# Attention scores over 128 rows, block adds tied together, and low parts of weight tiles on GpSimd

## The chip, the cores and the metric

The kernel runs on one core of one Trainium2 chip. The metric is the device time of one launch in microseconds (us). A core has TensorE (matrix products; PE in the profile, and PEld for its weight loads), VectorE (DVE), ScalarE (ACT), GpSimd (POOL) and SyncE (SP, which starts most transfers). Each runs its own list of instructions in order and waits for the others by semaphores.

## The reference

Two transformer blocks on 256 tokens of width 1024. The first adds three branches: a gated recurrence (lru), a sparse attention (nsa) and a gated linear attention (gla), then merges them and ends with an FFN. The second has two layers with a context of 256 more tokens; the even one has a windowed attention, the odd one a neighbourhood attention. All heads have 64 features.

```python
def nsa_mixer(q, kv, gate, rel_table, cmp_pos, cmp_w1, cmp_w2):
    ...
    blocks = jnp.concatenate([ch[:, :, j:j + n_cmp] for j in range(r)], axis=3) + pos_emb   # compress_blocks
    ...
    logit = jnp.einsum("bgrqd,bgqnld->bgrqnl", qb, ks).astype(f32) + bias
    ...
    logit_w = jnp.einsum("bgrnqd,bgnkd->bgrnqk", qw, kw).astype(f32) + bias_w
def rglru_mixer(...):
    u = jnp.sqrt(-jnp.expm1(2.0 * log_a)) * (i * xc.astype(f32))
    ...
    return h.astype(xa.dtype) * jax.nn.gelu(ga)
def window_gqa(q, k, v, k_ctx, v_ctx, sink):
    ...
    s_ctx = jnp.einsum('bnqkgd,bckd->bnkgqc', qb, k_ctx).astype(jnp.float32) * scale
def neighbourhood_attn(q, k, v, k_ctx, v_ctx, rpb):
    ...
    s_ctx = jnp.einsum('bmqhd,bchd->bhmqc', qr, k_ctx).astype(jnp.float32) * scale
```

## The kernel before

**Weights.** Every large product is done in three parts to keep float32 accuracy. `Core.wload` (L63) brings a weight tile of 128x1024 by a transfer on SP into `wraw`, ScalarE rounds it to `wh` (L74), and VectorE makes the low part `wl = wraw - wh` (L75). Each of the three has a ring of three buffers. `mm3` (L109) then issues `wh` x high, `wl` x high (L114, L115) and `wh` x low (L118) on TensorE. `wload` has an argument `low` for the engine of the subtraction; with none it is VectorE, and the subtraction is entered in `self.lows`, behind which the small adaLN products (L1131) are queued.

**Sparse attention.** `Block1.run` (L1006) weaves it with the recurrent branch: `K.weave(seq, nsa, NS)` runs a list of 44 projection units (each loads one weight tile: four of a gla output, sixteen of the two lru halves, sixteen merges, eight of a branch), and 0.83 steps of the attention after each. The attention has 32 items (8 chunks of heads x 2 query tiles x 2 heads). An item's step issues the score of item i (L645), the transposes of item i-2 (L667) and the values of item i-3 (L686). A score takes 64 of the 128 rows, since a chunk holds two heads:

```python
hs = slice(s * 64, s * 64 + 64)
nc.tensor.matmul(sps, self.qT[hs, ci, t * P:t * P + P], self.kT[hs, a, :, 0:nk], start=True, stop=True)
```

The keys `kT` are copied by ScalarE in `k_unit` (L489), long before. In an lru half GpSimd does the inner part of a gelu (L147 to L149) and a square (L783) per unit, and VectorE a convolution (L757, L760) and the products L784 and L786.

**Blocks.** `blocks` (L515) adds a position table to the tokens of the sparse attention's compressed keys in 8 VectorE additions of 128x8x15 for each of two calls (L526), rounds the result on ScalarE and takes the rest on VectorE. `K.fill(1)` in `run` issues one piece of the adaLN work ahead.

**Even and odd attention.** The even layer's scores (L1556) are 32 items, 16 with 512 keys and 16 with 256; the keys are turned on TensorE and copied by ScalarE (`turned_k`, L1517). The odd layer's (L1788) are 16 items with 512 keys; its queries are turned and copied (L1767). Both are woven with projection units; in the odd layer with 4 tiles of 1024 columns and 8 of 512.

**Order.** The instructions are issued in the order of the program, and a scheduler of the tile framework then orders each engine's list by dependencies, priorities and the rings' free buffers. The ring `a4` of `Block1` has 8 buffers, and holds among others the keys, the values, the block sums and the recurrence's arrays.

Of the kernel before, what the change touches and what calls it, by code (L numbers as in the profile page):

```python
# [14 lines left out]
P = 128  # L15
# [9 lines left out]
class Core:  # L25
    def __init__(self, tc, ctx, D):
        self.tc, self.nc, self.D = tc, tc.nc, D
        self.cp = ctx.enter_context(tc.tile_pool(name="const", bufs=1))
        self.yp = ctx.enter_context(tc.tile_pool(name="big", bufs=2))
        self.wp = ctx.enter_context(tc.tile_pool(name="wstream", bufs=3))  # L30
        self.sp = ctx.enter_context(tc.tile_pool(name="small", bufs=2))
        self.pp = ctx.enter_context(tc.tile_pool(name="psum", bufs=4, space=PSUM))
        self.n = 0
        self.ready, self.lows = {}, []

        self.filler, self.rate, self.credit = [], 0.0, 0.0
        nc = self.nc
        self.ident = self.cp.tile([P, P], F32, name="ident")
        nc.scalar.dma_start(self.ident, D["ident"])
        self.ones = self.cp.tile([P, P], F32, name="ones")  # L40
        nc.vector.memset(self.ones, 1.0)

        ps = self.psum("at")
        for _ in range(WARM):
            nc.tensor.matmul(ps[:, :P], self.ones, self.ones, start=True, stop=True)
        self.power = self.cp.tile([P, 8], F32, name="power")
        nc.gpsimd.memset(self.power, -0.5)
        self.ng = self.cp.tile([P, 32], F32, name="ng")
        nc.scalar.dma_start(self.ng, D["ng"])
# [11 lines left out]
                self.ready[key] = self.wload(src, src.shape[-1], False, low, parts)  # L61

    def wload(self, src, cols, take=True, low=None, parts=1):  # L63
        nc = self.nc
        key = src.tensor.name, src.offset
        if take and key in self.ready:
            return self.ready.pop(key)
        raw = self.wp.tile([P, 1024], F32, tag="wraw", name=self.nm("wraw"))
        h = self.wp.tile([P, 1024], F32R, tag="wh", name=self.nm("wh"))
        l = self.wp.tile([P, 1024], F32R, tag="wl", name=self.nm("wl"))  # L70
        for i in range(parts):
            c = slice(i * cols // parts, (i + 1) * cols // parts)
            nc.sync.dma_start(raw[:, c], src[:, c])
            nc.scalar.copy(h[:, c], raw[:, c])  # L74
            i = (low or nc.vector).tensor_tensor(out=l[:, c], in0=raw[:, c], in1=h.bitcast(F32)[:, c],  # L75
                                                 op=ALU.subtract)
        if low is None:
            self.lows = (self.lows + [i.ins.name])[-LOOSE:]
        self.credit += self.rate
        while self.credit >= 1.0:  # L80
            self.credit -= 1.0
            self.fill(1)
        return h, l
# [247 lines left out]
class Block1:  # L331
# [156 lines left out]

    def k_unit(self, br, a):  # L489
        if br == a == 0:  # L490
            self.kT = self.a4("kT", shape=(P, 2, 2, 256))
        self.nc.scalar.copy(self.kT[:, a, br, :], self.proj_t(12 + 2 * br + a))

    def v_units(self):
        self.vN = self.a4("vN", shape=(P, 2, 512))
# [19 lines left out]
    def blocks(self, kv):  # L515

        nc = self.nc
        x2r = self.x2[kv].rearrange("p g (c s) -> p s g c", s=16)
        flat = self.a4("blk", shape=(P, 1024))
        bh = self.a8("blkh", F32R, (P, 1024))  # L520
        bl = self.a8("blkl", F32R, (P, 1024))
        nc.gpsimd.memset(flat[:, 960:], 0.0)
        blk = flat[:, :960].rearrange("p (i g c) -> p i g c", i=16, g=4)
        for ih in range(2):
            for g in range(4):
                nc.vector.tensor_tensor(  # L526
                    out=blk[:, 8 * ih:8 * ih + 8, g, :], in0=x2r[:, 0::2, g, ih:ih + 15],
                    in1=self.cpos[:, kv, 8 * ih:8 * ih + 8][:, :, None].to_broadcast([P, 8, 15]), op=ALU.add)
        nc.scalar.copy(bh, flat)
        nc.vector.tensor_tensor(out=bl, in0=flat, in1=bh.bitcast(F32), op=ALU.subtract)  # L530
        self.blk.append((bh, bl))

# [71 lines left out]
    def nsa_steps(self):  # L604
# [35 lines left out]
        def scores(ci, t, s):  # L640
            a, r = divmod(ci, 4)
            g, nk = 2 * a + s, (t + 1) * P
            sps = K.psum("mm")[:, :2 * nk].rearrange("p (b n) -> p b n", b=2)
            hs = slice(s * 64, s * 64 + 64)
            nc.tensor.matmul(sps, self.qT[hs, ci, t * P:t * P + P], self.kT[hs, a, :, 0:nk], start=True, stop=True)  # L645
            pr = self.s1("t2", (P, 512)).rearrange("p (b n) -> p b n", b=2)[:, :, :nk]
            nc.vector.tensor_tensor(out=pr, in0=sps, in1=Bs[ci][:, s:s + 1, 256 - nk:].to_broadcast([P, 2, nk]),
                                    op=ALU.add)
            mx = self.s1("mx", (P, 2))
            nc.vector.tensor_reduce(out=mx, in_=pr, axis=AX.X, op=ALU.max)  # L650
            nc.vector.tensor_scalar(out=mx, in0=mx, scalar1=-1.0, scalar2=None, op0=ALU.mult)
            sm = self.s1("sm", (P, 2))
            for b in range(2):
                nc.scalar.activation(pr[:, b, :], pr[:, b, :], AF.Exp, bias=mx[:, b:b + 1], accum_out=sm[:, b:b + 1])
            nc.vector.reciprocal(sm, sm)
            nc.vector.tensor_tensor(out=sm, in0=sm, in1=gv[:, t, 1:3, g, r], op=ALU.mult)
            for b in range(2):
                nc.vector.tensor_scalar(out=pr[:, b, :], in0=pr[:, b, :], scalar1=sm[:, b:b + 1], scalar2=None,
                                        op0=ALU.mult)
            prs[ci, t, s] = pr  # L660
# [345 lines left out]
    def run(self):  # L1006
# [9 lines left out]
        k = [(lambda br=br, a=a: self.k_unit(br, a)) for br in range(2) for a in range(2)]  # L1016
        self.gates_turned()
        self.nsa_rows()
        K.fill(1)
        for f in q[2:5]:  # L1020
            f()
        self.blocks(0)
        for f in q[5:]:
            f()
        self.blocks(1)
        decay = self.gla_decay()

        def mixed(a, b):
# [50 lines left out]
        K.rate = 0.0  # L1079
        seq = b2[4:] + l0 + [then(l1[0], *a0)] + l1[1:] + [then(mg[0][0], *a1)] + mg[0][1:6]  # L1080
        seq += [then(mg[0][6], ysplit), mg[0][7]] + b0 + mg[1]
        K.weave(seq, nsa, NS)
        for _ in nsa:
            pass
        K.rate = RATE_GLA
# [141 lines left out]
class Block2:  # L1227
# [224 lines left out]
    def even(self, l, z, norm, ahead):  # L1452
# [50 lines left out]
        for f in self.proj_units(z, W[0:4], 512, X, to(q), z.steps(1)):  # L1503
            f()
        qT = K.big("qT", shape=(P, 4, 512))
        kT = self.t("kT", (P, 512))

        def turned_q(ts):
            for c in range(0, 4, 2):
# [7 lines left out]
        def turned_k(ts):  # L1517
            ps = K.psum("at")
            for n, t in enumerate(ts):
                nc.tensor.transpose(ps[:, n * P:n * P + P], k[:, t, :], K.ident)  # L1520
            nc.scalar.activation(kT[:, ts[0] * P:ts[-1] * P + P], ps[:, :len(ts) * P], AF.Copy,
                                 scale=1.0 if ts == X else gc[:, 1:2])

        def heads():
            yield from self.head_norm(q, X, 8)
# [25 lines left out]
        def score(item, pr):  # L1551
            t, keys, h = item
            c, s = divmod(h, 2)
            hs = slice(s * 64, s * 64 + 64)
            ps = K.psum("mm")[:, :len(keys) * P]
            nc.tensor.matmul(ps, qT[hs, c, t * P:(t + 1) * P], kT[hs, keys[0] * P:keys[-1] * P + P], start=True,  # L1556
                             stop=True)
            parts = [(ps[:, :256], mask[:, t, :]), (ps[:, 256:], None)] if t < 2 else [(ps, None)]
            return self.softmax(parts, (sink[:, h:h + 1], nsink[:, h:h + 1]), pr)
# [177 lines left out]
    def odd(self, l, z, norm, ahead):  # L1737
# [25 lines left out]
        K.weave(vu, heads(), 1)  # L1763
        kT = K.big("qT", shape=(P, 4, 512))
        self.to_T(k, 4, 4, lambda c, ps: nc.scalar.activation(kT[:, c, :], ps, AF.Copy, scale=gc[:, 1:2]))
        qT = self.t("e4", (P, 4, 256))
        self.to_T(q, 2, 4, lambda c, ps: nc.scalar.activation(qT[:, c, :], ps, AF.Copy, scale=gc[:, 0:1]))  # L1767
        y = (self.t("hh", (P, 8, 256), F32R), self.t("hl", (P, 8, 256), F32R))

        items = [(t, (0, 1, 2, 3), h) for t in range(2) for h in range(8)]  # L1770
# [8 lines left out]
        def score(item, pr):  # L1779
            t, keys, h = item  # L1780
            c, s = divmod(h, 2)
            hs = slice(s * 64, s * 64 + 64)
            if (t, c) not in Bs:
                bias(t, c)
            if s == 0 and t * 4 + c < 7:
                bias(*divmod(t * 4 + c + 1, 4))
            ps = K.psum("mm")
            nc.tensor.matmul(ps, qT[hs, c, t * P:(t + 1) * P], kT[hs, c, :], start=True, stop=True)  # L1788
            return self.softmax([(ps[:, :256], Bs[t, c][:, s, :]), (ps[:, 256:], None)], None, pr)
        prb = self.t("n8", (P, 4, 512), bufs=2)  # L1790
        ptb = self.t("wsT", (P, 2, 512))
# [3 lines left out]
        def pooled(g):  # L1795
# [13 lines left out]
            self.split_evac(y, g, 0, 256, t)  # L1809
            yield  # L1810
        pools = (None for g in range(4) for _ in pooled(g))
        K.weave(self.proj_units(z, W[12:16], 512, X, to(xp)), att, OD)
        K.weave([lambda: next(pools, None)] * 8 + self.out_units(l, K.D["od_o"], y, 256, range(4)), att, OD2)
        for _ in att:
            pass
        return self.out_proj(l, K.D["od_o"], y, 256, norm, ahead, range(4, 8))
# [312 lines left out]
```

## Time and profile before

| what | us |
|---|---|
| median of 3 runs (lowest to highest) | 2393.02 (2391.76 to 2394.91) |
| the profiled execution | 2392.35 |
| its span | 2390.6 |
| busy: TensorE | 2354.4 (98%) |
| busy: VectorE | 1710.8 (72%) |
| busy: ScalarE | 1051.4 (44%) |
| busy: GpSimd | 175.4 (7%) |

The span runs from the first instruction to the last, in one profiled execution; the execution's own time has 1.75 us more around it. The busy shares are averages over stages with different limits, so a stage is read from its own window. Matmuls overlap at their ends, so the distance between two starts tells what one takes, rather than its own duration. PEclk is the granted clock of TensorE, 1.00 for 2.4 GHz and 0.50 for 1.2 GHz.

### The profile page before, as it was taken

To read this page: it belongs to the slowest core of one execution; us is meant where nothing else is said; L and a number is where in the kernel's file an instruction comes from. 1 tells how busy PE (TensorE), PEld (TensorE's weight loads), DVE (VectorE), ACT (ScalarE), POOL (GpSimd) and SP (SyncE) were. 2 spreads that over 40 slices of the span, in tenths; PEclk is the share of its full clock that TensorE was granted. 3 is DMA by queue.
4 is the path that set the end of the run, shared out by engine and by line. 5 is a ranking of instruction groups with operands and counts; after the bars stand their busy time and mean duration, and the time that the engine had idled before them with its cause. 6 is when DMAs were issued, how large, how long until landed. Compare 5 with 4: busy or idle time off the path is not lost.

```text
span 2390.6 us, 38670 instructions
## 1 busy us (share of the span) xinstructions
PE 2354.4 (98%) x14647; PEld 2065.6 (86%) x14647; DVE 1710.8 (72%) x3621; ACT 1051.4 (44%) x1839; POOL 175.4 (7%) x203
## 2 busy tenths in 40 slices
PE   8999999999999999999999999999999999999999
PEld 8888988999999988888778888888988888878999
DVE  7976898789899964458767765656865643846666
ACT  5532576465445422236755322223522223656443
POOL 1000120010000000003321000000100000100000
PEclk9999999999999999999999999999999999999999
DMA  7773533567886755545214644544653532534554
GB/s 241 244 238 113 161 110 117 152 221 239 268 267 215 258 178 162 168 132 162 94 58 136 208 154 129 162 140 137 208 165 126 155 111 90 182 119 132 185 180 157
DMA packets 158310, 398.91 MB, mean 167 GB/s; under 512 B 27131, under 2 KB 41371, under 8 KB 158123
## 3 DMA queue, kind: packets, MB, share of 16 engines
q1 hardware_dynamic: 157835, 396.35, 52.8%
q8 instruction: 115, 1.88, 0.3%
q14 instruction: 72, 0.59, 0.1%
q10 hardware_dynamic: 288, 0.08, 0.0%
HBM read 389.56 MB, written 5.77 MB: 165 GB/s over the span
## 4 chain that ended last, share of the span: by engine, by line
PE 82%; DVE 8%; DMA 4%; ACT 2%; issue 2%; POOL 1%; SPq 0%; ACTq 0%; DVEq 0%; POOLq 0%
PE ps_mm L114 23%; PE ps_mm L118 22%; PE ps_mm L115 22%; DVE wl L75 3%; PE ps_mm L1315 2%; PE ps_mm L1316 2%; PE ps_mm L1317 2%; DMA wraw<-in_up 2%; DVE junk L1131 1%; PE ps_at L1422 1%; ACT wh L74 1%; PE ps_mm L645 1%; PE ps_mm L1556 1%; DMA wraw<-in_w_in_t 1%; PE ps_at L1411 1%
## 5 line engine op out<-in xcount | busy, mean ns | idle before, releaser
L74 ACT CAST wh<-wraw 128x1024 fp32r<-128x1024 f32 (+2 forms) x605 | 605.4, 1001 | 735.8 <-PE ps_mm L118 369.9
L75 DVE TENSOR_TENSOR wl<-wraw,wh 128x1024 fp32r<-128x1024 f32 (+2 forms) x605 | 707.5, 1170 | 264.3 <-ACT wh L74 248.6
L114 PE MATMUL ps_mm<-zh,wh 128*128 128x256 f32 (+2 forms) x2512 | 751.3, 324 | 7.2 <-ACT wh L74 5.9
L115 PE MATMUL ps_mm<-zh,wl 128*128 128x256 f32 (+2 forms) x2512 | 746.8, 322 | 6.5 <-DVE wl L75 6.4
L114 PEld LDWEIGHTS ps_mm<-zh,wh 128*128 128x128 f32 x2512 | 477.8, 190 | 62.4 <-issue 12.7
L115 PEld LDWEIGHTS ps_mm<-zh,wl 128*128 128x128 f32 x2512 | 478.3, 190 | 49.9 <-DVE wl L75 9.2
L118 PE MATMUL ps_mm<-zl,wh 128*128 128x256 f32 (+2 forms) x2512 | 448.0, 321 | 0.0
L118 PEld LDWEIGHTS ps_mm<-zl,wh 128*128 128x128 f32 x2512 | 373.7, 190 | 38.5 <-issue 0.3
L1131 DVE SCALAR_TENSOR_TENSOR junk<-araw,cs 128x512 f32<-128x512 f32 x576 | 391.4, 691 | 10.8 <-DMA araw<-in_ada_w 3.8
L114 PE MATMUL ps_mm<-hh,wh 128*128 128x256 f32 (+1 forms) x1021 | 313.0, 329 | 1.9 <-ACT wh L74 0.9
L115 PE MATMUL ps_mm<-hh,wl 128*128 128x256 f32 (+1 forms) x1021 | 311.3, 327 | 1.0 <-DVE wl L75 1.0
L114 PEld LDWEIGHTS ps_mm<-hh,wh 128*128 128x128 f32 x1021 | 192.8, 189 | 23.1 <-ACT hh L300 1.6
L115 PEld LDWEIGHTS ps_mm<-hh,wl 128*128 128x128 f32 x1021 | 193.0, 189 | 20.3 <-DVE wl L75 1.6
L118 PE MATMUL ps_mm<-hl,wh 128*128 128x256 f32 (+1 forms) x1021 | 194.1, 328 | 0.2 <-DVE hl L301 0.2
L118 PEld LDWEIGHTS ps_mm<-hl,wh 128*128 128x128 f32 x1021 | 156.6, 189 | 18.9 <-DVE hl L301 0.4
L298 ACT ACTIVATE silu<-ps_mm 128x512 f32<-128x512 f32 (+1 forms) x102 | 50.2, 493 | 261.1 <-PE ps_mm L118 242.7
L1261 DVE SCALAR_TENSOR_TENSOR X<-ps_mm,adac,X 128x256 f32<-128x256 f32 x128 | 61.9, 483 | 133.9 <-PE ps_mm L118 132.8
L299 DVE TENSOR_TENSOR silu<-silu,ps_mm 128x512 f32<-128x512 f32 (+1 forms) x102 | 56.6, 555 | 105.8 <-PE ps_mm L118 105.8
L126 POOL TENSOR_TENSOR rs_v<-rs_v,power 128x2 f32<-128x2 f32 (+1 forms) x17 | 24.1, 1418 | 1291.4 <-ACT wh L74 713.5
L1315 PE MATMUL ps_mm<-wh,zh 128*128 128x512 f32 (+1 forms) x224 | 87.3, 390 | 0.0
L1316 PE MATMUL ps_mm<-wh,zl 128*128 128x512 f32 (+1 forms) x224 | 86.0, 384 | 0.0
L1317 PE MATMUL ps_mm<-wl,zh 128*128 128x512 f32 (+1 forms) x224 | 85.6, 382 | 0.0
(399 smaller groups left out, 2661.2 us busy)
## 6 DMA issues: line engine op xcount, KB each, us to landing
wraw<-in_up SPq DMA_DIRECT2D x204, 512.0 KB, 3.7
araw<-in_ada_w SPq DMA_DIRECT2D x288, 256.0 KB, 3.4
wraw<-in_w_in_t SPq DMA_DIRECT2D x70, 512.0 KB, 3.6
wraw<-in_dn SPq DMA_DIRECT2D x79, 448.0 KB, 3.3
wraw<-in_f_up SPq DMA_DIRECT2D x44, 512.0 KB, 4.4
wraw<-in_dn SPq DMA_DIRECT2D x40, 512.0 KB, 3.6
wraw<-in_ev_in SPq DMA_DIRECT2D x26, 512.0 KB, 3.5
wraw<-in_w_br SPq DMA_DIRECT2D x24, 512.0 KB, 3.8
```

Source lines behind the costliest of these rows:

```text
L74: nc.scalar.copy(h[:, c], raw[:, c])
L75: i = (low or nc.vector).tensor_tensor(out=l[:, c], in0=raw[:, c], in1=h.bitcast(F32)[:, c], op=ALU.subtract)
L114: nc.tensor.matmul(out, wh, ah, start=start and k == 0, stop=False)
L115: nc.tensor.matmul(out, wl, ah, start=False, stop=False)
L118: nc.tensor.matmul(out, wh, al, start=False, stop=stop and k == n - 1)
L298: nc.scalar.activation(g, p0, AF.Silu)
L299: nc.vector.tensor_tensor(out=g, in0=g, in1=ps, op=ALU.mult)
L1131: K.behind(nc.vector.scalar_tensor_tensor(out=junk, in0=raw, scalar=1.0, in1=self.cs[:, s, h * 512:(h + 1) * 512], op0=ALU.mult, op1=ALU.mult,
L1261: self.nc.vector.scalar_tensor_tensor(out=X[:, m, :], in0=ps, scalar=self.ada.c[l][:, j, m, s:s + 1], in1=X[:, m, :], op0=ALU.mult, op1=AL ...
L1315: nc.tensor.matmul(ps[i], z.zh[:, k, tk], wh[:, w], start=k == 0, stop=False)
L1316: nc.tensor.matmul(ps[i], z.zl[:, k, tk], wh[:, w], start=False, stop=False)
L1317: nc.tensor.matmul(ps[i], z.zh[:, k, tk], wl[:, w], start=False, stop=k == 7)
```

## The change

Three edits. First, each score is a product over all 128 rows. One of the two operands exists twice, once for each head of the chunk, with zeros in the other head's 64 rows, so that the sum over 128 rows is the same. GpSimd writes the zeros. In the odd layer the queries are doubled, elsewhere the keys. Second, the 8 block additions of a call become 2 of 128x480, the rounding that follows is kept in its place in the program, and `K.fill(1)` comes after the blocks. Third, `Core.low` names the engine of the low parts: GpSimd while the sparse attention and the two weaves of the odd layer are issued, 44 and 12 tiles. Line numbers of the changed kernel are some 2 to 25 higher.

```diff
@@ wload
-        nc = self.nc
+        nc, low = self.nc, low or self.low
@@ k_unit
-            self.kT = self.a4("kT", shape=(P, 2, 2, 256))
-        self.nc.scalar.copy(self.kT[:, a, br, :], self.proj_t(12 + 2 * br + a))
+            self.kT = [self.a4("kT", shape=(P, 2, 2, 256)) for s in range(2)]
+            for s in range(2):
+                self.nc.gpsimd.memset(self.kT[s][(1 - s) * 64:(1 - s) * 64 + 64], 0.0)
+        ps = self.proj_t(12 + 2 * br + a)
+        for s in range(2):
+            hs = slice(s * 64, s * 64 + 64)
+            self.nc.scalar.copy(self.kT[s][hs, a, br, :], ps[hs])
@@ blocks
-            for g in range(4):
-                nc.vector.tensor_tensor(
-                    out=blk[:, 8 * ih:8 * ih + 8, g, :], in0=x2r[:, 0::2, g, ih:ih + 15],
-                    in1=self.cpos[:, kv, 8 * ih:8 * ih + 8][:, :, None].to_broadcast([P, 8, 15]), op=ALU.add)
-        nc.scalar.copy(bh, flat)
+            nc.vector.tensor_tensor(
+                out=blk[:, 8 * ih:8 * ih + 8], in0=x2r[:, 0::2, :, ih:ih + 15],
+                in1=self.cpos[:, kv, 8 * ih:8 * ih + 8][:, :, None, None].to_broadcast([P, 8, 4, 15]), op=ALU.add)
+
+        self.K.tc.keep_in_program_order(nc.scalar.copy(bh, flat))
@@ nsa_steps, scores
-            hs = slice(s * 64, s * 64 + 64)
-            nc.tensor.matmul(sps, self.qT[hs, ci, t * P:t * P + P], self.kT[hs, a, :, 0:nk], start=True, stop=True)
+            nc.tensor.matmul(sps, self.qT[:, ci, t * P:t * P + P], self.kT[s][:, a, :, 0:nk], start=True, stop=True)
@@ Block1.run
-        K.fill(1)
...
         self.blocks(1)
+        K.fill(1)
...
+        K.low = K.nc.gpsimd
         K.weave(seq, nsa, NS)
+        K.low = None
@@ even attention
-        kT = self.t("kT", (P, 512))
+        kT = [self.t("kT", (P, 512)), k.rearrange("p t n -> p (t n)")]
...
-            nc.scalar.activation(kT[:, ts[0] * P:ts[-1] * P + P], ps[:, :len(ts) * P], AF.Copy,
-                                 scale=1.0 if ts == X else gc[:, 1:2])
+            cols = slice(ts[0] * P, ts[-1] * P + P)
+            for s in range(2):
+                hs, other = slice(s * 64, s * 64 + 64), slice((1 - s) * 64, (1 - s) * 64 + 64)
+                nc.gpsimd.memset(kT[s][other, cols], 0.0)
+                nc.scalar.activation(kT[s][hs, cols], ps[hs, :len(ts) * P], AF.Copy,
+                                     scale=1.0 if ts == X else gc[hs, 1:2])
...
-            nc.tensor.matmul(ps, qT[hs, c, t * P:(t + 1) * P], kT[hs, keys[0] * P:keys[-1] * P + P], start=True,
+            nc.tensor.matmul(ps, qT[:, c, t * P:(t + 1) * P], kT[s][:, keys[0] * P:keys[-1] * P + P], start=True,
@@ odd attention
-        qT = self.t("e4", (P, 4, 256))
-        self.to_T(q, 2, 4, lambda c, ps: nc.scalar.activation(qT[:, c, :], ps, AF.Copy, scale=gc[:, 0:1]))
+        e4, ge = self.t("e4", (P, 4, 256)), [self.t("gelu", (P, 512), bufs=2) for _ in range(2)]
+        qT = [[e4[:, c, :] for c in range(4)], [ge[c // 2][:, c % 2 * 256:c % 2 * 256 + 256] for c in range(4)]]
+        nc.gpsimd.memset(e4[64:128], 0.0)
+        for g in ge:
+            nc.gpsimd.memset(g[0:64], 0.0)
+        def turned_q(c, ps):
+            for s in range(2):
+                hs = slice(s * 64, s * 64 + 64)
+                nc.scalar.activation(qT[s][c][hs], ps[hs], AF.Copy, scale=gc[hs, 0:1])
+        self.to_T(q, 2, 4, turned_q)
...
-            nc.tensor.matmul(ps, qT[hs, c, t * P:(t + 1) * P], kT[hs, c, :], start=True, stop=True)
+            nc.tensor.matmul(ps, qT[s][c][:, t * P:(t + 1) * P], kT[:, c, :], start=True, stop=True)
...
+        K.low = nc.gpsimd
         K.weave(self.proj_units(z, W[12:16], 512, X, to(xp)), att, OD)
         K.weave([lambda: next(pools, None)] * 8 + self.out_units(l, K.D["od_o"], y, 256, range(4)), att, OD2)
+        K.low = None
```

How the engines' lists change is shown at two places. The first is GpSimd's list in the first lru half, one unit; `t` is the unit's gelu, `lv` the square of the recurrence's factor, `lc` a buffer of the compressed scores. Before:

```order
L147 TENSOR_TENSOR t_606_3233<-t_601_3200 128x256
L754 MEMSET t_614_3266 128x4
L148 TENSOR_SCALAR t_606_3233<-t_606_3233 128x256
L149 TENSOR_TENSOR t_606_3233<-t_606_3233,t_601_3200 128x256
L621 MEMSET lc_3853 128x2x8
```

With the change, the same unit (L149 to L151 are now the gelu, L789 the square):

```order
L789 TENSOR_TENSOR lv_2983<-la_2984 128x256
L628 MEMSET lc_3848 128x2x8
L149 TENSOR_TENSOR t_607_3228<-t_602_3195 128x256
L760 MEMSET t_615_3261 128x4
L150 TENSOR_SCALAR t_607_3228<-t_607_3228 128x256
L151 TENSOR_TENSOR t_607_3228<-t_607_3228,t_602_3195 128x256
L77 TENSOR_TENSOR wl_3409<-wraw_3407,wh_3408 128x1024
L77 TENSOR_TENSOR wl_3513<-wraw_3511,wh_3512 128x1024
```

Two low parts, of tiles that TensorE uses two tiles later, stand behind each gelu, and the next unit's work behind them. The transfers into `wraw`, queued on SP, wait for GpSimd's readers of the buffer instead of VectorE's.

The second is VectorE's list in the second lru half; `lu` is the recurrence's input, `sm` and `t` with 128x256 x2 belong to a softmax, `convw` to the convolution. Before, the product L786 of a unit stands in the midst of it:

```order
L757 TENSOR_SCALAR t_709_3749<-t_704_3715,convw,lruv 128x256
L75 TENSOR_TENSOR wl_3886<-wraw_3884,wh_3885 128x1024
L655 RECIPROCAL sm_3708<-sm_3708 128x2
L760 SCALAR_TENSOR_TENSOR t_709_3749<-t_704_3715,convw,t_709_3749 128x256
L656 TENSOR_TENSOR sm_3708<-sm_3708,nsagate 128x2
L786 SCALAR_TENSOR_TENSOR lu_3556<-t_711_3757,t_680_3594 128x256
L658 TENSOR_SCALAR t_701_3703<-t_701_3703,sm_3708 128x256 x2
```

With the change the same products (now L792) of all four units stand together, after the last gelu of the half (L154):

```order
L154 SCALAR_TENSOR_TENSOR lg_3552<-t_781_4108,t_776_4075 128x256
L656 TENSOR_REDUCE mx_4127<-t_786_4125 128x2
L657 TENSOR_SCALAR mx_4127<-mx_4127 128x2
L661 RECIPROCAL sm_4130<-sm_4130 128x2
L662 TENSOR_TENSOR sm_4130<-sm_4130,nsagate 128x2
L664 TENSOR_SCALAR t_786_4125<-t_786_4125,sm_4130 128x256 x2
L792 SCALAR_TENSOR_TENSOR lu_3551<-t_712_3752,t_681_3589 128x256
L792 SCALAR_TENSOR_TENSOR lu_3551<-t_746_3919,t_710_3744 128x256
L792 SCALAR_TENSOR_TENSOR lu_3551<-t_767_4035,t_744_3911 128x256
L681 COPY pct_4197<-ps_at_4195 128x128
L792 SCALAR_TENSOR_TENSOR lu_3551<-t_795_4173,t_765_4027 128x256
```

The `wl` rows are gone from VectorE's list, and the four `lu` products moved behind the half's last gelu: the second `kT` holds a buffer of the ring `a4` that `lu` took before, so `lu` waits for another to come free. What the products read (`t`, buffers of the ring that the softmax uses too) is held until then.

## Rows read from the trace of the kernel before

**Rows 1.** Page, busy time of the engines, share of the span, instructions.

```profile
PE 2354.4 (98%) x14647; PEld 2065.6 (86%) x14647; DVE 1710.8 (72%) x3621; ACT 1051.4 (44%) x1839; POOL 175.4 (7%) x203
```

**Rows 2.** Windows: us; busy PE, PEld, DVE, ACT, POOL (instructions); PEclk, DMA, GB/s.

```profile
275.00:360.00 85.00, 83.16 (x592) 72.70 (x592) 79.38 (x214) 61.04 (x155) 26.18 (x42) 1.00 0.39 118
360.00:447.00 87.00, 86.67 (x642) 76.55 (x642) 70.96 (x200) 50.93 (x129) 7.21 (x10) 1.00 0.37 114
1130.00:1240.00 110.00, 107.72 (x544) 77.84 (x543) 73.16 (x236) 76.14 (x201) 37.52 (x34) 0.98 0.24 77
2115.00:2168.00 53.00, 53.00 (x282) 37.23 (x281) 24.38 (x95) 31.18 (x77) 0.00 (x0) 1.00 0.23 68
```

**Rows 3.** Timeline of PE: start, us, line, operation, out<-in, rows*columns, columns, number.

```profile
284.00 0.39 PE L683 MATMUL ps_at<-pct,vc 128*128 128x128 f32 x2
284.22 1.06 PE L686 MATMUL ps_at<-t,vN 128*128 128x128 f32 x8
285.21 0.70 PE L645 MATMUL ps_mm<-kT,qT 64*128 64x256 f32 x2
285.83 0.38 PE L114 MATMUL ps_mm<-zh,wh 128*128 128x256 f32 x1
```

**Rows 4.** Timeline of PE, 128 rows and 256 columns (lru gates).

```profile
333.97 1.02 PE L775 MATMUL ps_at<-t,lruw 128*128 128x256 f32 x4
334.83 0.38 PE L667 MATMUL ps_at<-ident,t 128*128 128x128 f32 x2
```

**Rows 5.** Timeline of PE, an even score of 512 columns.

```profile
1183.82 1.12 PE L1556 MATMUL ps_mm<-kT,qT 64*128 64x512 f32 x2
1184.87 0.50 PE L1315 MATMUL ps_mm<-wh,zh 128*128 128x512 f32 x1
```

**Rows 6.** Timeline of PEld, the weight load behind the score of rows 3.

```profile
285.83 0.19 PEld L114 LDWEIGHTS ps_mm<-zh,wh 128*128 128x128 f32 x1 [0.33 <-issue]
```

**Rows 7.** Source view, passes of the sparse and even scores: ns min/median/max, starts, forms.

```profile
L645 PE MATMUL ps_mm<-kT,qT x64: 376/534/693, 257.5 to 445.7; 64*128 64x256 f32 x32, 64*128 64x512 f32 x32
L1556 PE MATMUL ps_mm<-kT,qT x64: 376/534/693, 1130.9 to 1236.3; 64*128 64x256 f32 x32, 64*128 64x512 f32 x32
```

**Rows 8.** Groups by line and form: busy us, mean ns of one, idle time before.

```profile
L893 POOL MEMSET gatt<- 128x256 f32 x4 | 1.2, 312 | 76.8 <-PE ps_at L927 76.8
L492 ACT COPY kT<-ps_mm 128x256 f32<-128x256 f32 x4 | 1.5, 368 | 2.9 <-PE ps_mm L118 2.9
L1723 POOL TENSOR_TENSOR rpb<-rpb,amask 128x512 f32<-128x512 f32 x8 | 10.4, 1303 | 56.9 <-DMA rpb<-rpb_scratch 56.9
L201 POOL TENSOR_TENSOR zl<-zt,zh 128x256 fp32r<-128x256 f32 x48 | 51.0, 1064 | 97.3 <-ACT zh L200 85.7 <-issue 9.8 <-DVE hss L1337 1.7
```

**Rows 9.** Windows, the stretch with the blocks.

```profile
60.00:120.00 60.00, 56.05 (x361) 48.16 (x362) 54.38 (x120) 35.75 (x46) 5.78 (x7) 1.00 0.74 244
```

**Rows 10.** Windows, sparse score passes alone (L645): us, busy PE, PEld, clock, DMA.

```profile
275.00:360.00 85.00, 11.61 (x26) 3.83 (x26) 1.00 0.39 118
360.00:447.00 87.00, 13.85 (x30) 4.41 (x30) 1.00 0.37 114
```

**Rows 11.** Windows, VectorE's low parts alone (L75): us, busy DVE.

```profile
275.00:360.00 85.00, 19.96 (x16) 1.00 0.39 118
360.00:447.00 87.00, 20.91 (x18) 1.00 0.37 114
```

**Rows 12.** Timeline of POOL and DVE, L656 alone and beside a product of GpSimd.

```profile
333.12 0.16 DVE L656 TENSOR_TENSOR sm<-sm,nsagate 128x2 f32<-128x2 f32 x1
...
337.97 0.76 POOL L783 TENSOR_TENSOR lv<-la 128x256 f32<-128x256 f32 x1
338.15 0.59 DVE L656 TENSOR_TENSOR sm<-sm,nsagate 128x2 f32<-128x2 f32 x1
```

**Rows 13.** Windows around a fall of the granted clock.

```profile
1144.80:1148.20 3.40, 2.72 (x14) 1.51 (x12) 3.33 (x11) 2.00 (x5) 1.36 (x1) 1.00 0.11 16
1148.20:1151.60 3.40, 3.30 (x10) 2.82 (x11) 1.96 (x7) 2.09 (x9) 0.00 (x0) 0.50 0.53 193
```

More of the change, by code (lines that the diff above doesn't have):

```diff
@@ L34, in __init__ @@
         self.ready, self.lows = {}, []
+        self.low = None
         self.filler, self.rate, self.credit = [], 0.0, 0.0
@@ L1553, in score @@
             c, s = divmod(h, 2)
-            hs = slice(s * 64, s * 64 + 64)
             ps = K.psum("mm")[:, :len(keys) * P]
-            nc.tensor.matmul(ps, qT[hs, c, t * P:(t + 1) * P], kT[hs, keys[0] * P:keys[-1] * P + P], start=True,
+            nc.tensor.matmul(ps, qT[:, c, t * P:(t + 1) * P], kT[s][:, keys[0] * P:keys[-1] * P + P], start=True,
                              stop=True)
@@ L1781, in score @@
             c, s = divmod(h, 2)
-            hs = slice(s * 64, s * 64 + 64)
             if (t, c) not in Bs:
```

## The prediction

> **What bounds the kernel now.** I read the page's busy shares first. TensorE is at work for 98% of the span [rows 1], so a change pays if it shortens TensorE's own stream, or costs if another engine falls so far behind that TensorE has to wait. Second come the windows over the four stretches that the change touches [rows 2]. The sparse attention is 275 to 360 us (beside the recurrent branch, called the lru stretch here) and 360 to 447 us; the even layer's attention is 1130 to 1240 us and the odd layer's 2115 to 2168 us. TensorE is busy for 83.16 of 85, 86.67 of 87, 107.72 of 110 and all 53 us. The reader should also see who stands nearest behind it: in the lru stretch VectorE has 79.38 of 85 us, while GpSimd has only 26.18. In the other three there is room on both. So time saved on TensorE shows up in full in three stretches, and in the lru stretch as far as VectorE and GpSimd keep up.
>
> **Part 1: scores over 128 rows.** The work removed is the odd time that a 64-row matmul takes. A float32 matmul runs here as two passes, and the timeline shows them by their starts [rows 3]. Two L683 passes over 128 rows and 128 columns go from 284.00 to 284.22, 0.11 us each. The eight L686 passes behind them, of the same shape, need 0.99 us to the score's start at 285.21, so 0.11 more than 8 x 0.11: the first 64-row pass enters late. The two score passes of 256 columns then last to 285.83, 0.62 us. With 128 rows, four passes of 256 columns go from 333.97 to 334.83 [rows 4], 0.215 each, so two would take 0.43. A score of 256 columns thus loses 0.11 + 0.19 = 0.30 us; start times have two digits, so I take 0.29. With 512 columns the two passes last from 1183.82 to 1184.87, 1.05 us [rows 5]; at twice 0.215 each they would take 0.86, which saves 0.19, and I take the same entry. No 512-column float32 matmul over 128 rows stands in the rows, so the 0.86 is an estimate from rows 4. The cause is visible on the weight loads: the load behind the score stands idle for 0.33 us before it starts, which the profile calls issue [rows 6], whereas loads elsewhere run beside the matmul ahead.
>
> There are 64 such passes in the sparse and 64 in the even attention [rows 7], 32 scores each, and the odd layer's list of items has 16: 80 x 0.29 = **23.2 us** off TensorE's stream, 9.3 in each of the first two attentions and 4.6 in the odd one. TensorE's order of matmuls stays nearly as it was, and no pass is added.
>
> What it adds: the zero halves and more copies. The memsets go to GpSimd. 128x256 takes 0.31 us there [rows 8], so a 64x1024 half is at most some 1.25 us; two of them stand well ahead of the first sparse score, the odd layer's three are at most 2.5 us in a stretch where GpSimd has nothing [rows 2], and one 64x256 half (at most 0.31) stands between a turn of the even keys and its second score, a dozen projection matmuls later; those cover it, and without them it would cost 0.31 at each of the two turns. The sparse keys' four extra copies at 0.37 us [rows 8] go to ScalarE long before use. In the even layer each of the two turns now has two ScalarE copies where it had one, ahead of the first score: 0 to 2 x 0.37, and I take **+0.7**. In the odd layer four more copies, 0 to 1.5 us; the queries' first chunk is ready after two, so I take 0.
>
> **Part 2: the blocks.** Sixteen VectorE adds become four over the same number of columns, so VectorE loses only what an instruction costs beside its columns. VectorE is busy for 54.38 of the 60 us there, and TensorE idles for 60 - 56.05 = 3.95 [rows 9]: that caps a gain. Against it stand the ScalarE cast, now tied to its place in the program, and the filler that comes later; both are hidden while TensorE has units queued, and without that cover they cost one wait of the same size. I take 0, and -4 to +4 as ends.
>
> **Part 3: low parts on GpSimd.** VectorE loses 56 subtractions, 44 of them under the sparse attention. In the odd layer VectorE has 24.38 of 53 us and GpSimd nothing [rows 2], which leaves room for 12 tiles, so 0 there. In the lru stretch there are 16, in the next 18 [rows 11], and 26 and 30 score passes, 13 and 15 scores [rows 10]. A subtraction of 128x1024 on GpSimd doesn't occur. From below, twice the 128x512 product of L1723, 2 x 1.303 = 2.6 us; from above, four times the 128x256 difference rounded to the same type, L201, 4 x 1.064 = 4.26 [rows 8], a mean that includes waiting beside other work. VectorE takes 19.96 / 16 = 1.25.
> GpSimd keeps pace in the lru stretch up to (85 - 13 x 0.29 - 26.18) / 16 = 3.44 us, and in the next up to (87 - 15 x 0.29 - 7.21) / 18 = 4.19. I take 3.4, the middle, which costs nothing. Each subtraction is issued two tiles ahead of its use, 2 x 85 / 16 = 10.6 us, so its latency alone delays nobody.
> VectorE gets 79.38 - 19.96 = 59.4 us of work for 81.2. But the two engines hold each other up. L656, tiny, took 0.16 us alone and 0.59 when it started at 338.15 into a GpSimd product that ended at 338.73, 0.43 us of that product's 0.76, or 57% [rows 12]. For 16 subtractions the hold-up lies between 0 and the whole 2.6 us each, 0 to 41.6. At 57% it is 1.5 each, so VectorE comes to 59.4 + 24 = 83.4 against 81.2: **+2.2 us**, with 0 and +19.8 as ends. The four last products of the second lru half (L786) also come later, after the last gate; they hold ring buffers of the softmax, which nothing in the rows prices, and I count them inside that range.
>
> **Sum.** The profiled execution took 2392.35 us, 0.67 under the median of 2393.02, so they can be taken as one. 2392.35 - 23.2 + 0.7 + 2.2 = 2372.05: **2372.0 us**. A measurement of this kernel can tell some 0.2%, 4.8 us, from no change. The clock adds noise: from 1148.20 to 1151.60 it was granted at 0.50, the level of 1.2 GHz, after TensorE had been busy for 2.72 of the 3.4 us before [rows 13]. That costs up to half of 3.4, 1.7 us, and such a dip can come or go where waits shift.
>
> **Rivals.**
> *GpSimd is a little too slow.* At 4.26 us a subtraction it bounds the lru stretch by 16 x (4.26 - 3.44) = 13.1 us and the next by 18 x 0.07 = 1.3. Then 2392.35 - 23.2 + 0.7 + 14.4 = 2384.3. For it speaks that L201 is the same operation; against it that VectorE, which held L201 up, loses this very work.
> *The two engines take turns (slower).* If no VectorE instruction could run beside a GpSimd one, the lru stretch would need 59.4 + 26.2 + 41.6 = 127.2 us against 81.2, and the next 50.1 + 7.2 + 46.8 = 104.1 against 82.7: 46.0 + 21.4 more, 2392.35 - 22.5 + 67.4 = 2437.3. It decides once some 60% of VectorE's time has to stand alone (0.6 x 59.4 + 67.8 - 81.2 = 22.2, about what part 1 gives). The L656 row speaks for it; against it, the two engines' 79.4 + 26.2 us fitted into 85 before.
> The Trainium skill, "SBUF — State Buffer", section "SBUF: two separate sides", says that a GpSimd instruction and a VectorE instruction with two SBUF inputs lock a shared pair of ports in turn, the loser blocked for the whole instruction. By that rule L656 had to wait as its row shows, the trace agrees, but instructions that read PSUM would go on, so the turns would be partial and the time nearer to the first rival's.
> *Rows don't matter.* If the odd time belonged to something else than the 64 rows (waiting for data, say), no part of the 23.2 would come: 2392.35 + 0.7 = 2393.1, no change. Against it stands that the same gap follows every score, with 256 columns and with 512.
> The Trainium skill, "TensorE: Matmul & The Clock Gate", section "Step-by-step: what each phase is for", has it that load time goes by columns and that the row count doesn't matter, which would give this rival's time. The trace differs: 0.31 us a pass against 0.215 at the same 256 columns.
>
> **Chances.** Forecast (2362 to 2380) 0.72; GpSimd too slow (2380 to 2390) 0.15; rows don't matter 0.06; turns 0.05; under 2362 0.02. The range 2362 to 2386 takes in the bounds of part 2, the clock and two thirds of the first rival. Faster by over 0.2% (below 2388.2): 0.72 + 0.02 + 0.13 = 0.87. Within: 0.06 and the edge of the first rival, 0.08. Slower: 0.05.
>
> **What would show it.** The score passes stand 0.215 us apart with 256 columns and about 0.43 with 512, with no idle load behind them. The windows of the even and odd attention shrink by 9 and 5 us. In the lru stretch GpSimd is at 80 of 81 us or below, VectorE under 84. I am wrong if a subtraction takes over 3.5 us, if TensorE waits for wl on GpSimd, or if the 64-row gap stays.

## The result, and the profile after

The changed kernel takes 2422.2 us (2419.44 to 2425.13), the kernel before 2393.97 beside it: ratio 1.0124 [1.0106, 1.0142]. It is slower by 28 us where 21 less were forecast. The page of the changed kernel, busy time, answers to [rows 1]:

```profile
PE 2346.3 (97%) x14647; PEld 2078.7 (86%) x14647; DVE 1720.5 (71%) x3553; ACT 1055.3 (44%) x1849; POOL 302.7 (13%) x268
```

TensorE's busy time fell by 8 us and the span grew by 27: it waits. Both traces hold 14647 passes in nearly the same order, so a stage can be timed by the starts of the same passes. The table is worked out so, in us; idle is the sum of TensorE's gaps over 0.1 us.

| passes, stage | before | changed | low parts on GpSimd alone | scores and blocks alone | best run | best run with 64 rows |
|---|---|---|---|---|---|---|
| 0 to 250, start | 42.9 | 36.0 | 43.2 | 36.7 | 36.7 | 35.9 |
| 250 to 1750 | 219.7 | 225.7 | 219.7 | 225.5 | 228.5 | 221.6 |
| 1750 to 2500, sparse, mostly lru | 107.9 (idle 2.1) | 147.6 (32.9) | 147.2 (28.8) | 109.6 (9.2) | 104.7 (5.2) | 108.0 (2.4) |
| 2500 to 3250, sparse | 98.0 | 97.6 | 99.6 | 93.3 | 93.4 | 98.0 |
| 7500 to 8500, even | 195.0 (3.9) | 193.3 (9.7) | 194.4 (4.6) | 195.1 (9.1) | 182.3 (1.9) | 193.0 (2.4) |
| 12250 to 13000, odd | 136.9 | 133.2 | 138.2 | 133.3 | 133.3 | 136.9 |

Two windows of the changed kernel that answer to [rows 2] (the lru stretch is longer now):

```profile
264.00:387.00 123.00, 95.45 (x638) 87.00 (x637) 98.83 (x206) 61.69 (x157) 63.70 (x59) 0.86 0.27 85
1163.00:1272.00 109.00, 100.74 (x551) 79.41 (x552) 78.08 (x238) 77.08 (x204) 38.26 (x38) 0.98 0.25 79
```

In the lru stretch no engine is full: VectorE has 98.83 of 123 us, GpSimd 63.70. The waits of TensorE there, from 264 to 410 us (in total, times, longest):

```profile
PE ps_at L625 <- DVE pct L681: 14.1, 2, 8.3
PE ps_at L673 <- DVE t L664: 11.2, 3, 8.8
PE ps_at L625 <- ACT t L784: 3.4, 1, 3.4
PE ps_at L673 <- DVE pct L681: 3.4, 1, 3.4
PE ps_at L781 <- DVE t L766: 0.7, 1, 0.7
```

It waits for small results, most of them of VectorE: a copy of the compressed probabilities (L681), a scaling (L664). `wl` is not among them. The first long one in the timelines of GpSimd, VectorE and TensorE:

```profile
280.55 4.83 POOL L77 TENSOR_TENSOR wl<-wraw,wh 128x1024 fp32r<-128x1024 f32 x2
281.07 2.10 DVE L154 SCALAR_TENSOR_TENSOR lg<-t,t 128x256 f32<-128x256 f32 x1 [1.14 <-ACT t L153]
283.10 2.43 DVE L763 TENSOR_SCALAR t<-t,convw,lruv 128x256 f32<-128x256 f32 x1
285.63 1.17 DVE L766 SCALAR_TENSOR_TENSOR t<-t,convw,t 128x256 f32<-128x256 f32 x2
286.71 0.28 DVE L681 COPY pct<-ps_at 128x128 f32<-128x128 f32 x1
287.05 1.06 PE L625 MATMUL ps_at<-kcp,qT 128*128 128x30 f32 x4 [8.32 <-DVE pct L681]
```

Two subtractions follow each other on GpSimd for 4.83 us. L154 and L763, 0.4 us each where nothing holds them, end only when a subtraction ends, and L681 stands behind them. TensorE waits 8.32 us and then runs at half its clock. Windows around it:

```profile
278.70:287.05 8.35, 0.03 (x1) 0.00 (x1) 7.03 (x9) 4.77 (x10) 7.12 (x7) 0.67 0.32 97
287.05:291.50 4.45, 4.45 (x19) 4.27 (x20) 3.32 (x16) 0.70 (x3) 0.00 (x0) 0.50 0.25 93
291.50:296.00 4.50, 4.50 (x38) 4.45 (x38) 1.65 (x8) 2.93 (x8) 2.27 (x6) 0.97 0.00 0
```

In the 8.35 us with next to nothing to do the granted clock falls (0.67 in the mean), and behind them it stands at 0.50 (1.2 GHz): 19 passes in 4.45 us, against 38 in the next 4.50. So a wait is paid a second time.

The scores did become shorter. The timeline of TensorE in a later, undisturbed stretch answers to [rows 3]:

```profile
447.29 1.06 PE L692 MATMUL ps_at<-t,vN 128*128 128x128 f32 x8
448.18 0.60 PE L651 MATMUL ps_mm<-kT,qT 128*128 128x256 f32 x2
448.43 0.47 PE L116 MATMUL ps_mm<-yah,wh 128*128 128x256 f32 x1
448.73 0.28 PE L117 MATMUL ps_mm<-yah,wl 128*128 128x256 f32 x1
```

From the start of the eight passes to L117 it takes 1.44 us. In [rows 3] it is 1.61 to the start of L114. The matmuls behind that one, before:

```profile
286.06 0.28 PE L115 MATMUL ps_mm<-zh,wl 128*128 128x256 f32 x1
286.18 0.28 PE L114 MATMUL ps_mm<-zh,wh 128*128 128x256 f32 x1
```

L114, late itself, takes another 0.23 us before the next matmul starts at 286.06: 1.84 in all. So a score saves up to 0.40 us here, not 0.29.

### The profile page after: what moved, and what is told of

Its sections match the earlier page's. It is cut to its first block, busy times and chain, and to the rows that moved or that the text cites. A ratio compares the mean times of both kernels' runs of the same rounds, so it can differ in the third digit from the quotient of the medians.

```text
span 2417.7 us, 38684 instructions
## 1 busy us (share of the span) xinstructions
PE 2346.3 (97%) x14647; PEld 2078.7 (86%) x14647; DVE 1720.5 (71%) x3553; ACT 1055.3 (44%) x1849; POOL 302.7 (13%) x268
## 4 chain that ended last, share of the span: by engine, by line
PE 77%; DVE 13%; DMA 3%; ACT 3%; issue 2%; POOL 1%; SPq 0%; ACTq 0%; DVEq 0%; POOLq 0%
PE ps_mm L116 22%; PE ps_mm L117 22%; PE ps_mm L120 22%; DVE wl L77 3%; DVE junk L1139 2%; PE ps_mm L1324 2%; PE ps_mm L1323 2%; PE ps_mm L1325 2%; PE ps_at L1430 1%; DMA wraw<-in_up 1%; ACT wh L76 1%; DVE t L664 1%; ACT t L660 1%; PE ps_mm L913 1%; PE ps_mm L1568 1%
## 5 line engine op out<-in xcount | busy, mean ns | idle before, releaser
L77 DVE TENSOR_TENSOR wl<-wraw,wh 128x1024 fp32r<-128x1024 f32 (+2 forms) x549 | 643.7, 1174 | 239.5 <-ACT wh L76 232.5
L116 PE MATMUL ps_mm<-zh,wh 128*128 128x256 f32 (+2 forms) x2512 | 764.4, 328 | 2.1 <-DVE Xc L1269 1.1
L117 PE MATMUL ps_mm<-zh,wl 128*128 128x256 f32 (+2 forms) x2512 | 754.3, 324 | 7.7 <-DVE wl L77 7.6
L117 PEld LDWEIGHTS ps_mm<-zh,wl 128*128 128x128 f32 x2512 | 484.7, 193 | 55.2 <-DVE wl L77 10.9
L116 PEld LDWEIGHTS ps_mm<-zh,wh 128*128 128x128 f32 x2512 | 484.6, 193 | 48.7 <-issue 6.1
L117 PE MATMUL ps_mm<-hh,wl 128*128 128x256 f32 (+1 forms) x1021 | 310.5, 327 | 1.0 <-DVE wl L77 0.9
L117 PEld LDWEIGHTS ps_mm<-hh,wl 128*128 128x128 f32 x1021 | 192.3, 188 | 21.0 <-DVE wl L77 1.9
L77 POOL TENSOR_TENSOR wl<-wraw,wh 128x1024 fp32r<-128x1024 f32 (+1 forms) x56 | 128.7, 2304 | 150.4 <-ACT wh L76 145.4
L301 DVE TENSOR_TENSOR silu<-silu,ps_mm 128x512 f32<-128x512 f32 (+1 forms) x102 | 56.6, 555 | 104.7 <-PE ps_mm L120 104.7
```

The source lines that it names most:

```text
L116: nc.tensor.matmul(out, wh, ah, start=start and k == 0, stop=False)
L117: nc.tensor.matmul(out, wl, ah, start=False, stop=False)
L301: nc.vector.tensor_tensor(out=g, in0=g, in1=ps, op=ALU.mult)
```

## The experiments

**Which part.** Theory A: GpSimd's subtractions hold up VectorE's instructions, and TensorE waits for what stands behind them. Theory B: the ring `a4`, with one buffer less, makes it late. The first runs take the parts singly.

```diff
-        K.low = K.nc.gpsimd
         K.weave(seq, nsa, NS)
-        K.low = None
...
-        K.low = nc.gpsimd
         K.weave(self.proj_units(z, W[12:16], 512, X, to(xp)), att, OD)
```

> The changed kernel with all low parts back on VectorE; scores over 128 rows and the tied blocks stay. Theory A (GpSimd's subtraction holds up VectorE's instructions, VectorE's list comes late, TensorE waits and its clock falls): all of the loss goes, the scores' gain stays, 2392 - 23 + 1 = 2370 us, 2364 to 2378. Theory B (the second kT takes a buffer of the ring a4, and what stands behind that ring comes late): the loss stays, 2410 to 2425.

2381.03 us, ratio 0.9957 [0.9940, 0.9974]. The loss of 41 us goes, but of the scores' 23 us at most half has come. The kernel before with these lines added, and `wload`'s:

> The kernel before with the low parts on GpSimd in the same three weaves, nothing else. Theory A: the loss of the lru stretch without the scores' gain, 2392 + 40 + 5 to 10 = 2430 to 2450 us. Theory B: no loss, since kT is one tile as before, 2388 to 2398.

2432.89 us, 1.0171 [1.0142, 1.0200]: 41 us slower, 39.3 of them in the lru passes, and without a second `kT`. Theory B falls. 26.7 of the 39.3 are idle time (28.8 - 2.1). In the other 12.6 the passes take longer, as in the window at 0.50. Windows over the same lru passes, before and with the low parts alone; the second line of each pair has the low parts only (VectorE's before, then VectorE's and GpSimd's):

```profile
263.60:371.50 107.90, 105.73 (x753) 91.97 (x752) 97.71 (x267) 76.43 (x190) 26.44 (x43) 1.00 0.35 108
263.60:371.50 107.90, 22.99 (x20) 1.00 0.35 108
263.90:411.10 147.20, 118.37 (x753) 102.56 (x752) 117.15 (x249) 75.97 (x187) 72.84 (x64) 0.87 0.29 83
263.90:411.10 147.20, 0.00 (x0) 52.32 (x21) 0.87 0.29 83
```

The same passes keep TensorE busy for 118.37 us in place of 105.73, at a granted clock of 0.87 in place of 1.00. VectorE, rid of its low parts, is busy for 117.15 us in place of 97.71 - 22.99 = 74.7: 42 us of hold-up, 2.0 us for each of 21 subtractions.

The scores alone, part 2 alone (the block additions with the later `K.fill(1)`), and the later `K.fill(1)` alone, each on the kernel before:

> The kernel before with the scores over 128 rows alone. If the tied blocks cost or give nothing (as forecast) the time is that of the run without low parts on GpSimd within 3 us, 2366 to 2378. If the 5 us by which the changed kernel is ahead at 40 to 190 us come from the blocks, this run is 5 us longer than that one.

> The kernel before with the tied block additions and the later filler alone. Forecast: 0, so 2388 to 2396 us. If the early lead of the changed kernel is theirs: 2386 to 2389. If the falls of the clock at 187 to 224 us are theirs: 2394 to 2400.

> The kernel before with the one piece of adaLN work issued after the blocks, the block additions as they were. If the 4.7 us of the run with the tied blocks come from that piece (its transfers no longer compete with the first weights): 2385 to 2389. If they come from the additions: 2390 to 2394.

Scores 2389.5 us, 0.9988 [0.9972, 1.0003]; part 2 2387.27, 0.9979 [0.9964, 0.9993]; fill 2388.63, 0.9988 [0.9973, 1.0003]. The scores by themselves gave nothing that can be told from no change. Part 2 is worth some 5 us. It shortens the first 250 passes by 6 us (table), and this is the fill's: with the later fill alone they take 35.5 us, and TensorE's waits there for `wh` on ScalarE fall from 5.7 to 0.6 us. The additions run at 30 to 46 us in the trace of before, not in the stretch of [rows 9]; what they give by themselves stays open. Where the start is shorter, most or all of that gain is lost again before pass 1750, except in the last column, in falls of the clock that differ from one profiled execution to the next: between passes 250 and 1750 it is granted at 0.50 for 3.4 us before, for 13.7 in the changed kernel and for 27.3 in the best run. Why isn't shown.

**How GpSimd costs.** All on the changed kernel. First the lru units on VectorE again:

```diff
+        def lru(f):
+            def g():
+                K.low = None
+                f()
+                K.low = K.nc.gpsimd
+            return g
+        l0, l1 = [lru(f) for f in l0], [lru(f) for f in l1]
```

> The changed kernel with the 16 tiles of the recurrent branch's units on VectorE again; the 28 others of the sparse attention and the 12 of the odd layer stay on GpSimd. Theory A (hold-ups that matter are in the lru stretch, where VectorE has no room): 2381 us as without any low part on GpSimd, at most 8 more from the other stretch, 2380 to 2390. If GpSimd's low parts cost the same wherever they stand: a third of the 41 us goes, some 2407.

2400.82 us, 1.0039 [1.0024, 1.0055]. The 28 other tiles cost some 20 us, nearer to the second expectation (2407), though VectorE has room beside most of them. Room in an engine's sum is not what counts. Then L681 on ScalarE, `nc.scalar.copy(pcts[ci, t], tp)`:

> The changed kernel with one VectorE copy of 0.28 us per query tile (L681, the compressed probabilities) on ScalarE. Theory A in its form as latency (what costs is that small results which TensorE awaits stand in VectorE's list behind held instructions): the waits for L681, 17.5 us, mostly go, with the falls of the clock behind them, 2395 to 2410. If the loss is VectorE's total load: 16 x 0.28 = 4.5 us at most, 2417 to 2422.

2424.65 us, 1.0148 [1.0123, 1.0173]. That is over both expectations, and a miss for the narrow form of theory A: TensorE waited at the same places, now for L664 (12.4 us) and ScalarE's L784 (15.2). All that stands behind the held instructions is late, not one copy. Then the subtraction in pieces, and memsets in its place (the low parts of these tiles are left out):

```diff
-            i = (low or nc.vector).tensor_tensor(out=l[:, c], in0=raw[:, c], in1=h.bitcast(F32)[:, c],
-                                                 op=ALU.subtract)
+            n = 4 if (low or nc.vector) is nc.gpsimd else 1
+            m = cols // parts // n
+            for x in range(n):
+                d = slice(c.start + x * m, c.start + (x + 1) * m)
+                o = (low or nc.vector).tensor_tensor(out=l[:, d], in0=raw[:, d], in1=h.bitcast(F32)[:, d],
+                                                     op=ALU.subtract)
+            i = o
```

> The changed kernel with each of GpSimd's subtractions in four pieces of a quarter of the columns. If the pair is held for one instruction and goes to the other engine then: VectorE waits at most a piece, 0.65 us, in place of 2.1 to 2.5, and most of the loss goes, 2385 to 2400. If GpSimd keeps it as long as it has work: 2415 to 2430.

```diff
-            i = (low or nc.vector).tensor_tensor(out=l[:, c], in0=raw[:, c], in1=h.bitcast(F32)[:, c],
-                                                 op=ALU.subtract)
+            if (low or nc.vector) is nc.gpsimd:
+                nc.gpsimd.memset(l.bitcast(F32)[:, c], 0.0)
+                i = nc.gpsimd.memset(l.bitcast(F32)[:, c], 0.0)
+            else:
+                i = nc.vector.tensor_tensor(out=l[:, c], in0=raw[:, c], in1=h.bitcast(F32)[:, c],
+                                            op=ALU.subtract)
```

> The changed kernel with two memsets of the same 128x1024 tile in place of each GpSimd subtraction (the low parts of these tiles are left out, as zeros). GpSimd is occupied for about as long, 2 x 1.25 us, but reads nothing. Theory A (the two engines exclude each other where both read): no hold-up on VectorE, 2368 to 2381. Theory C (GpSimd's own gelu and squares come late behind the low parts): the loss stays, 2410 to 2425.

Pieces 2404.56 us, 1.0054 [1.0030, 1.0078], 5 us over the range for a hold-up of one instruction; memsets 2388.2, 1.0001 [0.9985, 1.0016], 7 us over theory A's range and 22 under theory C's. The groups of the gelu's last product on VectorE, 262 to 400 us, in the changed kernel, with pieces (the line is L159 there), with memsets (L158), and with all low parts on VectorE:

```profile
L154 DVE SCALAR_TENSOR_TENSOR lg<-t,t 128x256 f32<-128x256 f32 x8 | 13.6, 1702 | 5.6 <-ACT t L153 5.6
```

```profile
L159 DVE SCALAR_TENSOR_TENSOR lg<-t,t 128x256 f32<-128x256 f32 x8 | 4.3, 536 | 5.6 <-ACT t L158 5.6
```

```profile
L158 DVE SCALAR_TENSOR_TENSOR lg<-t,t 128x256 f32<-128x256 f32 x8 | 3.4, 423 | 7.8 <-ACT t L157 7.8
```

```profile
L154 DVE SCALAR_TENSOR_TENSOR lg<-t,t 128x256 f32<-128x256 f32 x8 | 3.4, 419 | 2.3 <-ACT t L153 2.3
```

1702 ns beside whole subtractions, 536 beside pieces, 423 beside memsets, 419 without. So the hold-up ends with GpSimd's instruction, and a memset, which reads nothing, doesn't hold this product. It does hold L763 (L767 there), which reads one tensor, with memsets and then with all low parts on VectorE:

```profile
L767 DVE TENSOR_SCALAR t<-t,convw,lruv 128x256 f32<-128x256 f32 x8 | 5.7, 716 | 0.0
L763 DVE TENSOR_SCALAR t<-t,convw,lruv 128x256 f32<-128x256 f32 x8 | 3.2, 404 | 0.0
```

A memset took 0.95 us, so GpSimd was occupied for 1.9 us a tile, less than meant; and some 7 us of the loss stay.

GpSimd's low parts in the odd layer alone:

> The changed kernel with GpSimd's low parts in the odd layer alone (12 tiles). Both forecast and theory A: nothing, as without any, 2378 to 2384. If a low part on GpSimd costs the same wherever it stands (some 0.7 us a tile): 2387 to 2392.

2384.42 us, 0.9965 [0.9949, 0.9980], against 0.9957 without any: nothing that can be told, as forecast.

**Where the scores' gain went.** With all low parts on VectorE the even passes take 195.1 us, as before, with 9.1 us idle in place of 3.9. One of these waits in that run's timelines (GpSimd, VectorE, ScalarE, TensorE):

```profile
1186.88 5.75 POOL L1353 TENSOR_TENSOR n<-n,bvg 128x512 f32<-128x512 f32 x3
1189.58 1.91 DVE L77 TENSOR_TENSOR wl<-wraw,wh 128x1024 fp32r<-128x1024 f32 x1
1191.41 1.77 DVE L154 SCALAR_TENSOR_TENSOR n8u<-gelu,n8u 128x512 f32<-128x512 f32 x1
1195.95 0.72 ACT L1392 ACTIVATE n<-n,smx 128x512 f32<-128x512 f32 x1 [3.19 <-DVE smx L1388]
1196.81 0.68 PE L1417 MATMUL ps_at<-ident,n 128*128 128x128 f32 x4 [2.30 <-ACT n L1392]
```

It is the same hold-up, by work of GpSimd that was there before: the `bvg` products stretch `wl` and a gelu's product, and the softmax behind them is late for a TensorE that now comes earlier. First VectorE is relieved in the sparse attention (L763 and every second L664 go to ScalarE), on the run without low parts on GpSimd and on the kernel before:

> Scores over 128 rows and tied blocks, all low parts on VectorE (2381 us), and two VectorE operations of the sparse attention's stretch go to ScalarE: the convolution's first product (8 x 0.41 us) and every second scaling of the probabilities (32 x 0.27 to 0.35). Theory D (without the scores' odd time VectorE's list becomes what TensorE waits for in the lru stretch): the waits there, 8 us, and the falls of the clock behind them go, 2370 to 2376. If the missing gain sits elsewhere: 2379 to 2384.

> The kernel before with the same two operations on ScalarE. Theory D: TensorE waited for VectorE for only some 2 us there, so 2388 to 2393. If VectorE's list already bounded the stretch: 2380 to 2386.

2376.06 us, 0.9947 [0.9928, 0.9965], and 2392.94, 1.0012 [1.0000, 1.0025]. By these times the relief can't be told from nothing (0.9957 [0.9940, 0.9974] without it); for theory D speaks only that the lru passes shrink by 3 us in the profiled execution (109.6 to 106.7), and that on the kernel before there is no gain. Then the `bvg` products go to VectorE, and in a further run the gelu's squares to ScalarE:

```diff
-                nc.gpsimd.tensor_tensor(out=xv, in0=xv, in1=gain, op=ALU.mult)
+                nc.vector.tensor_tensor(out=xv, in0=xv, in1=gain, op=ALU.mult)
...
-        nc.gpsimd.tensor_tensor(out=tmp, in0=x, in1=x, op=ALU.mult)
+        nc.scalar.activation(tmp, x, AF.Square)
```

> The kernel of the relief run (2376 us) with the even layer's four gain products of 128x512 on VectorE in place of GpSimd. Theory A for the even attention (GpSimd's products hold VectorE's list just ahead of a softmax): the wait of 2.3 us and the fall of the clock behind it, some 5 us, go, 2368 to 2373. Theory E (the softmax chain has its own pace, and TensorE now comes too early): VectorE has 2.7 us more to do, 2375 to 2380.

> The same, and the square that begins each gelu (GpSimd, 0.67 us for 256 columns, 1.04 for 512) on ScalarE. Theory A: fewer hold-ups in the even attention and in the lru stretch, another 1 to 5 us, 2366 to 2372. Theory E: ScalarE, at 70 to 80% in both stretches, becomes late: 2376 to 2384.

2374.92 us, 0.9933 [0.9918, 0.9947], and **2360.16 us, 0.9870 [0.9854, 0.9886]**, the fastest of all. The first is 1 us under the relief alone, inside the noise and between the two expectations; but the wait of 2.30 us shown above is gone, and the even passes take 190.0 us. The second is 6 us below the lower end that theory A gave. TensorE's waits in the even attention, 1125 to 1270 us, with the relief alone and then in the best run:

```profile
PE ps_at L1416 <- ACT n L1391: 4.5, 3, 2.3
PE ps_at L1427 <- ACT ysb L1428: 2.4, 2, 2.2
PE ps_at L1526 <- DVE e L1349: 1.6, 1, 1.6
PE ps_mm L1565 <- ACT qT L1521: 0.2, 1, 0.2
```

```profile
PE ps_at L185 <- POOL rs_v L128: 0.4, 1, 0.4
PE ps_at L1427 <- ACT ysb L1428: 0.2, 1, 0.2
```

The even passes fall from 195.1 to 182.3 us. VectorE's hold-ups are not the whole cause. The longest wait that is left once the `bvg` products are on VectorE, in the timelines of GpSimd, ScalarE and TensorE:

```profile
1137.84 1.59 POOL L151 TENSOR_TENSOR gelu<-gelu,n 128x512 f32<-128x512 f32 x1
1139.46 0.63 ACT L153 ACTIVATE gelu<-gelu 128x512 f32<-128x512 f32 x1 [1.52 <-POOL gelu L151]
1141.20 0.32 ACT L1428 ACTIVATE ysb<-ps_at,smx 128x64 f32<-128x64 f32 x1
1141.57 0.66 PE L1427 MATMUL ps_at<-e,rpb 128*128 128x64 f32 x4 [2.22 <-ACT ysb L1428]
```

Here ScalarE, whose list is in order too, waits for GpSimd's part of a gelu, and `ysb`, further back in its list, is late. With the square off GpSimd that part of the gelu is shorter, and the waits for `ysb` are down to 0.2 us in all. How the 15 us of the last edit divide between this and fewer hold-ups isn't shown. The last run puts the 64-row scores back into the best one:

> The kernel of 2360 us with the scores over 64 rows as before; blocks, relief, gain product and squares as there. Theory A (the scores' 23 us were there, and hold-ups took them back): 2360 + 23 = 2383, 2379 to 2387. If the other edits make the gain by themselves: 2362 to 2374.

2380.58 us, 0.9962 [0.9945, 0.9979]. The scores are worth 20 us once these waits are gone, 10.7 of them in the even passes (193.0 - 182.3).

## Why the prediction was wrong

*Part 1, 23.2 us.* The size was nearly right for TensorE's stream: 20 us between the last two runs. The step that failed is "time saved on TensorE shows up in full in three stretches". It was read from busy shares. In the even attention none of the 9.3 us arrived in the run without low parts on GpSimd: 5 us of new waits, for the softmax and for ScalarE behind a gelu, and slower passes (10.2 us at the granted clock 0.50 in place of 3.4) took it back. The lru passes of that run took 1.7 us more than before, not less. The odd layer gave 3.6 of 4.6 us and the later sparse passes 4.7, as counted on.

*Part 3, +2.2 us.* It cost 41 by itself. The bound of GpSimd's own speed was sound: a subtraction of 128x1024 took 2.475 us on average, under the lower bound of 2.6, and GpSimd kept pace. The failed step is "VectorE comes to 59.4 + 24 = 83.4 against 81.2", in two ways. First, the 24 is too small. The 57% behind it were misread: L656 started 0.18 us into GpSimd's product and ended with it, at 338.74 against 338.73 [rows 12], so it was held for all that was left. The runs showed 2.0 us a subtraction where 1.5 was taken; with that the prediction's sum gives 59.4 + 32 = 91.4 against 81.2, some 10 us. Second, the larger part: it is a sum of work over a stretch, as if work could be late anywhere in it. VectorE's list is in order, and TensorE needs results out of its midst two items later. The subtractions are issued right behind a gelu, met the products that follow the gelu, and held them to the end of a subtraction: L154 and L763 took 2.10 and 2.43 us in place of 0.4. VectorE was busy for 80% of the stretch and still late. The 12.6 us that are not idle time came with the granted clock, 0.87 in the mean in place of 1.00, which the prediction counted as noise of up to 1.7 us.

*The rivals.* Turns was nearest, with a chance of 0.05: right mechanism and side, but its price of 2437 let no VectorE instruction run beside GpSimd's, and it put the decision at 60% of VectorE's time standing alone, a sum again. The Trainium skill, "SBUF — State Buffer", section "SBUF: two separate sides", names whom the shared ports hold: VectorE instructions with two SBUF inputs, against GpSimd instructions that read SBUF, and those in a two-port mode. The trace agrees: L154, with two inputs, was held by subtractions and not by memsets. The prediction quoted this rule and took from it only that the turns would be partial. The other two rivals were wrong: GpSimd was not too slow, and the rows did matter. What the prediction set beside the last of them from the Trainium skill, "TensorE: Matmul & The Clock Gate", section "Step-by-step: what each phase is for", is said there of weight loads. For them the trace agrees: a load of 64 rows (L645) took 184 ns and one of 128 rows (L114) 190. The 0.31 us are of the matmul pass, so they don't speak against it.

*Part 2, 0.* Some 5 us faster by itself, just outside the bounds of -4 to +4. The cap was read from a stretch in which the additions don't run, and the later filler, which the prediction took as hidden or as a cost, shortened the start.

## What to carry to other kernels

Don't price a move from VectorE to GpSimd by busy shares: look at which VectorE instructions stand beside the moved one, how long they can be held (here to the end of GpSimd's instruction), and who waits for the results behind them. A gain on the busiest engine has to be followed to the next result it waits for, which here was late because of GpSimd work that had cost little before. And a wait of TensorE costs more than itself where its granted clock falls behind it.

## What the runs showed of the hardware that was not expected

A 64-row matmul delays its neighbour on both sides: 0.11 us at its entry, and the 128-row matmul behind it takes 0.23 us to the next start where 0.12 is usual [rows 3]. Behind a wait of 8.35 us the granted clock stood at 0.50 for another 4.45 us. GpSimd's memsets, which read nothing, held VectorE's L763 (716 ns in place of 404) and not its L154 (423 against 419). And GpSimd's memsets of 128x1024 took 0.95 us, three times the 0.31 of 128x256 for four times the columns [rows 8].
